# A decoder layer: weight and bias of the second layer norm applied by ScalarE on the transposed rows, and a written order from the cross-attention output to the first feed-forward group

## The chip, the cores and the metric

The kernel runs on one core of a Trainium2 chip. A core has a matrix engine (TensorE, PE in the profile, with PEld for its weight loads), VectorE (DVE), ScalarE (ACT), GpSimd (POOL) and SyncE (SP), which here issues the DMA transfers. Each engine works through its own queue in order; semaphores hold an instruction until what it reads is there. On chip there are SBUF, with 128 partitions, and PSUM, eight banks of 128 x 512 words, into which PE accumulates. The metric is the device time of one execution in microseconds (us), lower is better.

## What is computed

One layer of a decoder: a token mixer, a cross-attention, a feed-forward part, each followed by a layer norm over the sum with the scaled input. There are 256 tokens of 2048 features, all in float32.

```python
ALPHA = (2 * DEPTH) ** 0.25                       # DEPTH = 1
def layer_norm(x, g, b):
    mu = x.mean(-1, keepdims=True)
    var = jnp.square(x - mu).mean(-1, keepdims=True)
    return (x - mu) * lax.rsqrt(var + LN_EPS) * g + b

proj = x @ w_in                                   # 2048 -> 7176 columns
y = concat([mlstm_mixer(...), dilated_attention(...)]) @ w_out
x = layer_norm(ALPHA * x + y, ln_g[0], ln_b[0])
y = memory_cross_attention(x, mem, xq, xk, xv, xo)     # ends in o @ xo
x = layer_norm(ALPHA * x + y, ln_g[1], ln_b[1])
y = (silu(x @ w1) * (x @ w3)) @ w2                # hidden width 5632
x = layer_norm(ALPHA * x + y, ln_g[2], ln_b[2])
```

The change is about the second norm: the step from `o @ xo` to `x @ w1` and `x @ w3`.

## The kernel before, in words

**Products.** Each float32 factor is split into a high part (a cast to PE's fp32r, by ACT) and a low part (the difference to the original, by DVE): `split`, L109. A product is then three PE instructions: high by high, high by low part, low by high. One row of weights (a k-tile, 128 of the 2048 input features) is 128 x 1024; for a pair of rows one DMA brings a tile `w` (three of them in a ring, `RAW`), and the parts `wh`, `wl` go into rings of five (`SPLIT`) or into one of 34 numbered slots (`big`, given back by `free`). For 256 tokens (two halves m = 0, 1) and 1024 columns (two banks c) a row takes 2 x 6 products.

**gemm_seven** (L323) multiplies blocks with seven products in place of eight (sums of blocks are formed by `sums`, and `early` combines what they give). At its end it comes back to the `kept` rows: their products of the second token half are done last, so that the sums of the first half can begin sooner. **gemm_tokens** (L260) is the plain form, used for f0, the first 512 + 512 columns of w1 and w3. There the first six rows (`HEAD`) lie in slots, and the low parts of these are formed by POOL, in halves of 512 columns; PE does their products of token half 0, then those of half 1, and goes on with the others.

**The passage.** The output product of the cross-attention goes into z in two column halves, xo0 and xo1. `z[m][c]` are the rows (128 tokens x 512 columns, eight tiles; some of them have other names in the profile, such as `xk1r`). `Norm.add` adds a bank to z and takes the statistics, `Norm.finish` (L712) makes mean and scale (POOL does the power of -1/2), then two passes over the four tiles of z: L723 `(z - mean) * g`, L728 `* scale + b`. `put_transposed` (L735) then turns each tile into a PSUM bank (`x2p`) with four transposes (L739) and splits it into the operand `x2`, features by tokens: a cast by ACT, a difference by DVE (both L110/L111). z itself stays, as the input that the feed-forward part is added to much later (`w2_first`, L984, with scale ALPHA).

**After it.** f0's results go through `hidden` (L954: silu, product, transposes into `hT`); then come groups f2, f4, ... f20, each a `gemm_seven` over `x2`, whose results are put together by `whole` (L693, lines L696) before `hidden` takes them.

**Order.** Around the passage nothing is written by hand: the instructions of an engine are put in order by the framework's scheduler, which goes by a model of durations and by the buffers' rings. At the start of the program the same holds for the first stage, v0 (values of the mixer), beside which SP issues sixteen gathers of `rows`, a table of position biases.

Of the kernel before, what the change touches and what calls it, by code (L numbers as in the profile page):

```python
# [36 lines left out]
LAG, HEAD, LAG2 = 6, 6, 8  # L37
# [13 lines left out]
def decoder_layer(ctx: ExitStack, tc: tile.TileContext, A):  # L51
# [176 lines left out]
    def weights(src, n, name, load=None, kept=()):  # L228

        for b in range(n // 2):  # L230
# [13 lines left out]
            for i in range(2):  # L244
                at = 2 * b + i
                if load and n < KT:
                    load(at)
                if at in kept:
                    wh, wl = big(f"{name}h{at}"), big(f"{name}l{at}")
                else:  # L250
                    wh = wp.tile([P, W], F32R, tag="wh", name=f"{name}h{at}")
                    wl = wp.tile([P, W], F32R, tag="wl", name=f"{name}l{at}")
                eng = G if at in kept and kept[0] == 0 else V
                halves = (slice(0, 512), slice(512, 1024))
                for cs in halves if at in kept or first and i == 0 else (slice(0, 1024),):
                    SC.copy(wh[:, cs], w[:, i, cs])  # L256
                    eng.tensor_tensor(out=wl[:, cs], in0=w[:, i, cs], in1=as_f32(wh[:, cs]), op=ALU.subtract)  # L257
                yield at, wh, wl

    def gemm_tokens(op, src, nkt, name, order=None, kept=range(0), load=None, last=False):  # L260

        banks = [[bank(f"{name}b{m}{c}") for c in range(2)] for m in range(2)]
        order = order or list(range(nkt))

        def products(m, n, wh, wl, cols=range(2)):
            xh, xl = (op.get(order[n], x, m * P, P) for x in (0, 1))
            for c in cols:  # L270
                cs = slice(c * 512, (c + 1) * 512)
                T.matmul(banks[m][c], xh, wh[:, cs], start=n == 0, stop=False)  # L272
                T.matmul(banks[m][c], xh, wl[:, cs], start=False, stop=False)  # L273
            for c in cols:
                cs = slice(c * 512, (c + 1) * 512)
                T.matmul(banks[m][c], xl, wh[:, cs], start=False, stop=n == nkt - 1)  # L276

        behind = []
        for n, wh, wl in weights(src, nkt, name, load, kept):
            products(0, n, wh, wl)  # L280
            if n in kept:
                behind.append((n, wh, wl))
            else:
                products(1, n, wh, wl)
            if kept and n == kept[-1]:
                for c in range(2):
                    for i, wh, wl in behind:
                        products(1, i, wh, wl, (c,))
                for _, wh, wl in behind:
                    free(wh, wl)  # L290
            if last and n % 2 and n not in kept:
                op.free(order[n] // 2)
        if last:
            for n in kept:
                if n % 2:
                    op.free(order[n] // 2)
        return banks
# [25 lines left out]
    def gemm_seven(op, get, nkt, name, plan, early, order=None, kept=range(0), last=False):  # L323
# [49 lines left out]
        for c in range(2):  # L373
            for n, wh, wl in behind:
                tile_products(1, n, wh, wl, (c,))
        for n, wh, wl in behind:
            free(wh, wl)
            if last and n % 2:
                op.free(order[n] // 2)
# [272 lines left out]
    def add(m, g, banks, scale=ALPHA):  # L652
        for c in range(2):
# [39 lines left out]
    def whole(rows, banks):  # L693
        for m in range(2):
            for c in range(2):
                V.tensor_tensor(out=rows[m][c], in0=rows[m][c], in1=banks[m][c], op=ALU.add)  # L696

    class Norm:
# [7 lines left out]
        def add(self, m, g, banks, stats=True, scale=ALPHA):  # L706
            add(m, g, banks, scale)
            if stats:
                for c in (2 * g, 2 * g + 1):
                    V.bn_stats(out=self.st[m][:, c], in_=z[m][c])  # L710

        def finish(self, m, stats=False):  # L712
            if stats:
                for c in range(4):
                    V.bn_stats(out=self.st[m][:, c], in_=z[m][c])
# [4 lines left out]
            G.tensor_tensor(out=r[:, 1:2], in0=r[:, 0:1], in1=mhalf, op=ALU.pow)  # L720
            for c in range(4):
                t = z[m][c]
                V.scalar_tensor_tensor(  # L723
                    out=t, in0=t, scalar=mv[:, 0:1], in1=self.g[c], op0=ALU.subtract, op1=ALU.mult
                )
            for c in range(4):
                t = z[m][c]
                V.scalar_tensor_tensor(  # L728
                    out=t, in0=t, scalar=r[:, 1:2], in1=self.b[c], op0=ALU.mult, op1=ALU.add
                )  # L730

# [3 lines left out]
    def put_transposed(op, j0, m, t, name):  # L735

        pt = sbank(f"{name}p{j0}{m}")
        for i in range(4):
            T.transpose(pt[:, i * P : (i + 1) * P], t[:, i * P : (i + 1) * P], ident)  # L739
        for j in range(2):  # L740
            hi, lo = (x[:, :, m * P : (m + 1) * P] for x in op.views(j0 + j))
            split(hi, lo, pt[:, j * S : (j + 1) * S].rearrange("p (s t) -> p s t", s=2))
# [25 lines left out]
    nc.sync.dma_start(out=sel, in_=A["sel"])  # L768
    cw = const.tile([P, 16, 5], F32, tag="cw", name="cw")
# [350 lines left out]
```

## Time and profile before

| what | value |
|---|---|
| device time, median of 3 runs | 1546.54 us (1546.26 to 1547.52) |
| the profiled execution | 1546.63 us |
| its span, first to last instruction | 1544.8 us |
| instructions | 19283 |
| mean granted clock of PE | 0.995 |

The profile is that of one execution. A line of a timeline gives the start and the duration in microseconds, the engine, the source line and what is written from what, with the count of instructions that it stands for; in brackets is the idle time before it and what ended that. PE's durations overlap: a product counts from its start to its modelled end, and the next one starts before that. A line of a list of waits gives, after the colon, the time in total, the number and the longest. In a group line stand the least, the median and the greatest duration in ns. A granted clock of 1.00 is PE at full speed.

### The profile page before, as it was taken

The page shows a single profiled execution, that of the slowest core. Times are in us where ns is not written, and L with a number is a line of the kernel's source. Part 1 is how long each engine was busy: PE and PEld are TensorE (multiplying, and loading weights), DVE is VectorE, ACT ScalarE, POOL GpSimd, SP SyncE. Part 2 cuts the span into 40 slices and gives each one's busy share as a digit, 9 for nine tenths or more (in the row PEclk, how much of TensorE's full clock was granted, in tenths as well). Part 3 has the DMA queues.
Part 4 walks back from the last instruction along what each step waited for, and adds up shares of the span by engine and source line. Part 5 has one row for each costly group of instructions (what it writes and reads, how often), then busy time and mean ns, then how long its engine had stood idle before and what let it go on. Part 6 is the DMA issues. An engine that isn't in the chain of part 4 may idle for free.

```text
span 1544.8 us, 19283 instructions
## 1 busy us (share of the span) xinstructions
PE 1526.1 (99%) x7410; PEld 1277.2 (83%) x7410; DVE 1192.9 (77%) x1584; ACT 775.7 (50%) x1011; POOL 30.9 (2%) x30
## 2 busy tenths in 40 slices
PE   9999999999999999999999999999999999999997
PEld 7888888888888888888887888887788888888885
DVE  7665888787789655557788678887788878888897
ACT  5445555554544544444544554555445455555551
POOL 0000000000000000000014000000000000000000
PEclk9999999999999999999999999999999999999999
DMA  8674445674664546445553565665465656668552
GB/s 302 215 266 162 151 171 207 221 256 144 228 214 168 212 169 215 167 139 193 187 191 136 171 210 191 217 193 192 162 218 192 206 191 193 199 193 268 197 189 108
DMA packets 83354, 301.35 MB, mean 195 GB/s; under 512 B 7181, under 2 KB 9402, under 8 KB 59710
## 3 DMA queue, kind: packets, MB, share of 16 engines
q1 hardware_dynamic: 83262, 300.12, 56.3%
q8 instruction: 58, 0.95, 0.2%
q14 instruction: 34, 0.28, 0.1%
HBM read 297.97 MB, written 4.21 MB: 196 GB/s over the span
## 4 chain that ended last, share of the span: by engine, by line
PE 95%; DVE 3%; DMA 1%; issue 1%; ACT 0%; SPq 0%; DVEq 0%; ACTq 0%
PE w2a1P L338 2%; PE w2a0P L338 2%; PE w2b0P L338 2%; PE w2b1P L338 2%; PE f10P L338 2%; PE f20P L338 2%; PE v1P L338 2%; PE xo0P L338 2%; PE xo1P L338 2%; PE v0P L338 1%; PE f18P L338 1%; PE f8P L338 1%; PE wo0P L338 1%; PE f4P L338 1%; PE f2P L338 1%; PE f6P L338 1%
## 5 line engine op out<-in xcount | busy, mean ns | idle before, releaser
L257 DVE TENSOR_TENSOR xv1l<-xv1w,xv1h 128x1024 fp32r<-128x1024 f32 x16 | 19.6, 1224 | 20.7 <-ACT xv1h L256 20.6
L257 DVE TENSOR_TENSOR xv0l<-xv0w,xv0h 128x1024 fp32r<-128x1024 f32 x16 | 19.6, 1225 | 20.0 <-ACT xv0h L256 20.0
L110 ACT CAST w2a1h<-w2a1w 128x1024 fp32r<-128x1024 f32 (+1 forms) x24 | 22.5, 980 | 23.3 <-PE w2a1E L338 14.5
L110 ACT CAST w2a0h<-w2a0w 128x1024 fp32r<-128x1024 f32 (+1 forms) x24 | 22.8, 980 | 17.8 <-PE w2a0E L338 10.7
L111 DVE TENSOR_TENSOR w2a0l<-w2a0w,w2a0h 128x1024 fp32r<-128x1024 f32 (+1 forms) x24 | 26.5, 1131 | 6.1 <-ACT w2a0h L110 6.1
L111 DVE TENSOR_TENSOR w2a1l<-w2a1w,w2a1h 128x1024 fp32r<-128x1024 f32 (+1 forms) x24 | 26.4, 1131 | 5.6 <-ACT w2a1h L110 5.6
L256 ACT CAST xv1h<-xv1w 128x1024 fp32r<-128x1024 f32 x16 | 16.9, 1055 | 23.8 <-PE xv1b L276 17.2
L256 ACT CAST xv0h<-xv0w 128x1024 fp32r<-128x1024 f32 x16 | 16.9, 1055 | 21.6 <-PE xv0b L276 16.4
L110 ACT CAST w2b0h<-w2b0w 128x1024 fp32r<-128x1024 f32 (+1 forms) x20 | 19.2, 988 | 16.8 <-PE w2b0E L338 10.1
L338 PE MATMUL w2a0P<-w2a0h,hT 128*128 128x512 f32 x80 | 26.2, 391 | 0.2 <-ACT w2a0h L110 0.2
L257 POOL TENSOR_TENSOR f0l<-f0w,f0h 128x512 fp32r<-128x512 f32 x12 | 20.0, 1696 | 314.6 <-ACT f0h L256 314.6
L110 ACT CAST w2b1h<-w2b1w 128x512 fp32r<-128x512 f32 (+1 forms) x28 | 19.8, 758 | 12.5 <-PE w2b0E L338 5.4
L338 PE MATMUL w2a1P<-w2a1h,hT 128*128 128x512 f32 x80 | 25.4, 389 | 0.0
L110 ACT CAST wo1h<-wo1w 128x1024 fp32r<-128x1024 f32 (+1 forms) x16 | 15.6, 1000 | 18.9 <-PE wo1E L338 11.3
L110 ACT CAST f12h<-f12w 128x1024 fp32r<-128x1024 f32 (+1 forms) x16 | 15.6, 1000 | 18.7 <-PE f12E L338 11.3
L273 PE MATMUL f0b<-f0l,x 128*128 128x512 f32 x64 | 24.9, 405 | 0.1
L273 PE MATMUL xv0b<-xv0l,mT 128*128 128x512 f32 x64 | 25.0, 391 | 0.0
L111 DVE TENSOR_TENSOR w2b0l<-w2b0w,w2b0h 128x1024 fp32r<-128x1024 f32 (+1 forms) x20 | 22.2, 1139 | 3.6 <-ACT w2b0h L110 3.6
L272 PE MATMUL xv1b<-xv1h,mT 128*128 128x512 f32 x64 | 24.9, 392 | 0.0
L272 PE MATMUL xv0b<-xv0h,mT 128*128 128x512 f32 x64 | 24.9, 389 | 0.0
L273 PE MATMUL xv1b<-xv1l,mT 128*128 128x512 f32 x64 | 24.9, 389 | 0.0
L272 PE MATMUL f0b<-f0h,x 128*128 128x512 f32 x64 | 24.7, 407 | 0.0
(1641 smaller groups left out, 5488.4 us busy)
## 6 DMA issues: line engine op xcount, KB each, us to landing
w2a0w<-in_w SPq DMA_DIRECT2D x12, 1024.0 KB, 4.9
w2a1w<-in_w SPq DMA_DIRECT2D x12, 1024.0 KB, 5.2
w2b0w<-in_w SPq DMA_DIRECT2D x10, 1024.0 KB, 4.9
w2b1w<-in_w SPq DMA_DIRECT2D x10, 1024.0 KB, 5.0
v0w<-in_w_v SPq DMA_DIRECT2D x8, 1024.0 KB, 5.2
v1w<-in_w_v SPq DMA_DIRECT2D x8, 1024.0 KB, 4.9
v2w<-in_w_v SPq DMA_DIRECT2D x8, 1024.0 KB, 4.9
wo0w<-in_w_out SPq DMA_DIRECT2D x8, 1024.0 KB, 6.0
```

The source lines that it names most:

```text
L110: SC.copy(hi, src)
L111: V.tensor_tensor(out=lo, in0=src, in1=as_f32(hi), op=ALU.subtract)
L256: SC.copy(wh[:, cs], w[:, i, cs])
L257: eng.tensor_tensor(out=wl[:, cs], in0=w[:, i, cs], in1=as_f32(wh[:, cs]), op=ALU.subtract)
L272: T.matmul(banks[m][c], xh, wh[:, cs], start=n == 0, stop=False)
L273: T.matmul(banks[m][c], xh, wl[:, cs], start=False, stop=False)
L338: T.matmul(of[to], lhsT, rhs, start=to not in begun, stop=end)
```

## The change

- **Norm.** `Norm.bare` normalises z in one pass (`(z - mean) * scale`, one DVE instruction per tile). A small tile `lt` holds g and b with the features on the partitions; it is made at the start of the program by two loads, two PE transposes and a DVE copy. `scaled` lets ACT apply `lt` to the transposed tile, four activations of 128 x 128 from PSUM into a slot; ACT casts from there, and DVE takes the difference.
- **z.** Since z is then without g and b, `Norm.rest` multiplies and adds them on z later: 16 DVE instructions, which are to be issued after the last sum of `whole` of group f2.
- **Passage.** From the end of xo1 to f0's eighth row the order of PE, DVE and ACT is written by hand (`manual_schedule`). `gemm_seven` hands back the products of its kept rows as a generator (`behind`; a step is three products) so that the transposes can be put among them. The head has 8 rows, five of them in the rings. POOL has no subtractions any more.

The diff, cut to its core:

```diff
-LAG, HEAD, LAG2 = 6, 6, 8
+LAG, HEAD, POOLED, LAG2 = 6, 8, 5, 8
...
-                if at in kept:
-                    wh, wl = big(f"{name}h{at}"), big(f"{name}l{at}")
-                else:
-                    wh = wp.tile([P, W], F32R, tag="wh", name=f"{name}h{at}")
-                    wl = wp.tile([P, W], F32R, tag="wl", name=f"{name}l{at}")
-                eng = G if at in kept and kept[0] == 0 else V
+                wh = wp.tile([P, W], F32R, tag="wh", name=f"{name}h{at}")
+                wl = wp.tile([P, W], F32R, tag="wl", name=f"{name}l{at}")
                 halves = (slice(0, 512), slice(512, 1024))
-                for cs in halves if at in kept or first and i == 0 else (slice(0, 1024),):
-                    SC.copy(wh[:, cs], w[:, i, cs])
-                    eng.tensor_tensor(out=wl[:, cs], in0=w[:, i, cs], in1=as_f32(wh[:, cs]), op=ALU.subtract)
+                for cs in halves if first and i == 0 else (slice(0, 1024),):
+                    split(wh[:, cs], wl[:, cs], w[:, i, cs])
...
+    def token_products(op, banks, m, n, wh, wl, end):
+        xh, xl = (op.get(n, x, m * P, P) for x in (0, 1))
+        for c in range(2):
+            cs = slice(c * 512, (c + 1) * 512)
+            T.matmul(banks[m][c], xh, wh[:, cs], start=n == 0, stop=False)
+            T.matmul(banks[m][c], xh, wl[:, cs], start=False, stop=False)
+        for c in range(2):
+            cs = slice(c * 512, (c + 1) * 512)
+            T.matmul(banks[m][c], xl, wh[:, cs], start=False, stop=end)
+    def token_banks(name):
+        return [[bank(f"{name}b{m}{c}") for c in range(2)] for m in range(2)]
...
+        def rest():
+            for c in range(2):
+                for n, wh, wl in behind:
+                    yield tile_products(1, n, wh, wl, (c,))
             for n, wh, wl in behind:
-                tile_products(1, n, wh, wl, (c,))
-        for n, wh, wl in behind:
-            free(wh, wl)
-            if last and n % 2:
-                op.free(order[n] // 2)
+                free(wh, wl)
+                if last and n % 2:
+                    op.free(order[n] // 2)
+        if leave:
+            return banks, rest()
...
+        def bare(self, m, scales):
+            for t in z[m]:
+                V.tensor_scalar(
+                    out=t, in0=t, scalar1=scales[0], scalar2=scales[1], op0=ALU.subtract, op1=ALU.mult
                 )
+        def rest(self):
+            for c in range(4):
+                for m in range(2):
+                    t = z[m][c]
+                    V.tensor_tensor(out=t, in0=t, in1=self.g[c], op=ALU.mult)
+                    V.tensor_tensor(out=t, in0=t, in1=self.b[c], op=ALU.add)
...
+    def turn(m, t, name):
+        pt = sbank(name)
         for i in range(4):
             T.transpose(pt[:, i * P : (i + 1) * P], t[:, i * P : (i + 1) * P], ident)
+        return pt
+    def scaled(pt, j0, cols, name):
+        y = slot(name)
+        for i in range(4):
+            kt = 2 * j0 + i
+            SC.activation(
+                y[:, i * P : (i + 1) * P], pt[:, i * P : (i + 1) * P], ACT.Identity,
+                scale=cols[:, 0, kt : kt + 1], bias=cols[:, 1, kt : kt + 1],
+            )
+        return y
+    def parts_of(op, j0, m, y):
         for j in range(2):
             hi, lo = (x[:, :, m * P : (m + 1) * P] for x in op.views(j0 + j))
-            split(hi, lo, pt[:, j * S : (j + 1) * S].rearrange("p (s t) -> p s t", s=2))
+            yield hi, lo, y[:, j * S : (j + 1) * S].rearrange("p (s t) -> p s t", s=2)
...
+    lt, lrow, lp = const.tile([P, 2, KT], F32, tag="lt", name="lt"), slot("lrow"), sbank("ltp")
+    for i, x in enumerate(("ln_g", "ln_b")):
+        rows = lrow[:KT, i * P : (i + 1) * P]
+        nc.sync.dma_start(out=rows, in_=A[x][1].rearrange("c (i p) -> (c i) p", p=P))
+        T.transpose(lp[:, i * KT : (i + 1) * KT], rows, ident[:KT, :KT])
+    V.tensor_copy(lt.rearrange("p a k -> p (a k)"), lp[:, : 2 * KT])
+    free(lrow)
...
-    banks = gemm_seven(oT, fetch(A["xo"][1], "xo1"), KT, "xo1", plan, into_z(1, ALPHA), None, kept, True)
+    banks, behind = gemm_seven(
+        oT, fetch(A["xo"][1], "xo1"), KT, "xo1", plan, into_z(1, ALPHA), None, kept, True, leave=True
+    )
     x2 = Operand("x2")
-    for m in range(2):
-        ln.add(m, 1, banks, scale=1.0)
-        ln.finish(m)
-        for c in range(4):
-            put_transposed(x2, 2 * c, m, z[m][c], "x2")
-    ln.end()
+    f0, w0 = fetch(A["w13_tokens"], "f0"), {}
+    def upper(n):
+        if n % 2 == 0:
+            w0[n // 2] = f0(n // 2)
+        if n < POOLED:
+            wh, wl = (wp.tile([P, W], F32R, tag=f"w{x}", name=f"f0{x}{n}") for x in "hl")
+        else:
+            wh, wl = big(f"f0h{n}"), big(f"f0l{n}")
+        SC.copy(wh, w0[n // 2][:, n % 2])
+        return wh, wl
+    def lower(n):
+        wh, wl = head[n]
+        V.tensor_tensor(out=wl, in0=w0[n // 2][:, n % 2], in1=as_f32(wh), op=ALU.subtract)
+    def normal(m, c):
+        y = scaled(turns.pop((m, c)), 2 * c, lt, f"x2y{m}{c}")
+        p = list(parts_of(x2, 2 * c, m, y))
+        for hi, _, v in p:
+            SC.copy(hi, v)
+        ys[m, c] = y, p
+    def normal_low(m, c):
+        y, p = ys.pop((m, c))
+        for hi, lo, v in p:
+            V.tensor_tensor(out=lo, in0=v, in1=as_f32(hi), op=ALU.subtract)
+        free(y)
+    def step(n=1):
+        for _ in range(n):
+            next(behind, None)
+    def turn_in(m, c):
+        turns[m, c] = turn(m, z[m][c], f"x2p{m}{c}")
+    def head_products(m, *ns):
+        for n in ns:
+            token_products(x2, banks0, m, n, *head[n], False)
+    head, turns, ys = {}, {}, {}
+    with tc.manual_schedule(engines={mybir.EngineType.PE, mybir.EngineType.DVE, mybir.EngineType.Activation}):
+        for n in range(POOLED):
+            head[n] = upper(n)
+        for n in range(3):
+            lower(n)
+        step(6)
+        for c in range(2):
+            add(0, 1, banks, 1.0, (c,))
+            ln.stats(0, 2 + c)
+        r0 = ln.scales(0)
+        add(1, 1, banks, 1.0, (0,))
+        ln.stats(1, 2)
+        ln.bare(0, r0)
+        lower(3)
+        step(3)
+        for c in range(3):
+            turn_in(0, c)
+            step()
+            normal(0, c)
+        step(1)
+        normal_low(0, 0)
+        add(1, 1, banks, 1.0, (1,))
+        ln.stats(1, 3)
+        r1 = ln.scales(1)
+        normal_low(0, 1)
+        ln.bare(1, r1)
+        turn_in(0, 3)
+        banks0 = token_banks("f0")
+        head_products(0, 0, 1, 2)
+        lower(4)
+        turn_in(1, 0)
+        normal(1, 0)
+        normal_low(0, 2)
+        head[5] = upper(5)
+        head_products(0, 3, 4)
+        turn_in(1, 1)
+        normal(1, 1)
+        normal_low(1, 0)
+        lower(5)
+        normal(0, 3)
+        normal_low(1, 1)
+        normal_low(0, 3)
+        head_products(0, 5)
+        for n in (6, 7):
+            head[n] = upper(n)
+            lower(n)
+        turn_in(1, 2)
+        normal(1, 2)
+        normal_low(1, 2)
+        head_products(0, 6, 7)
+        turn_in(1, 3)
+        normal(1, 3)
+        normal_low(1, 3)
+        head_products(1, *range(HEAD))
+    for n in range(POOLED, HEAD):
+        free(*head[n])
+    for b in range(HEAD // 2, KT // 2):
+        for n, wh, wl in plain(f0, b, "f0"):
+            for m in range(2):
+                token_products(x2, banks0, m, n, wh, wl, n == KT - 1)
...
-    banks = gemm_tokens(x2, A["w13_tokens"], KT, "f0", kept=range(HEAD))
-    hidden(0, banks, lambda b, i: [x[:, i * 256 : (i + 1) * 256] for x in b], "f0")
+    hidden(0, banks0, lambda b, i: [x[:, i * 256 : (i + 1) * 256] for x in b], "f0")
...
+        done = whole(rows, banks)
         hidden(g, rows, lambda b, i: [b[i][:, x * 256 : (x + 1) * 256] for x in range(2)], f"f{g}")
         free(*rows[0], *rows[1])
+        if g == 2:
+            with tc.issue_after(done.ins):
+                ln.rest()
+            ln.end()
```

Three places of the order, each before and after, show what moves.

DVE at the end of group f2 (f2r, f2t and f2ru are its rows that are being put together; f4w, f4h, f4l the weights of the next group, their high and low parts), before:

```order
L962 TENSOR_TENSOR f2r_7660<-f2r_7660,x2r_7412 128x256
L696 TENSOR_TENSOR f2r_7660<-f2r_7660,f2E 128x512
L111 TENSOR_TENSOR f4l_7861<-f4w_7852,f4h_7860 128x512
L962 TENSOR_TENSOR f2t_7750<-f2t_7750,f2ru 128x256
L962 TENSOR_TENSOR f2r_7661<-f2r_7661,f2ru 128x256
L962 TENSOR_TENSOR f2t_7750<-f2t_7750,f2r_7660 128x256
L111 TENSOR_TENSOR f4l_7868<-f4w_7852,f4h_7867 128x1024
```

and after, where xk1r and z are tiles of z, xe and l1g in L736 the weight g, l1g and l1b in L737 the bias b:

```order
L684 TENSOR_TENSOR f2r_7689<-f2r_7689,f2E 128x512
L736 TENSOR_TENSOR xk1r_3523<-xk1r_3523,xe_6266 128x512
L736 TENSOR_TENSOR z_3535<-z_3535,xe_6266 128x512
...
L736 TENSOR_TENSOR z_3534<-z_3534,l1g_6312 128x512
L736 TENSOR_TENSOR z_3536<-z_3536,l1g_6312 128x512
...
L111 TENSOR_TENSOR f4l_7906<-f4w_7897,f4h_7905 128x512
L1091 TENSOR_TENSOR f2t_7779<-f2t_7779,f2ru 128x256
...
L737 TENSOR_TENSOR z_3534<-z_3534,l1b_6318 128x512
L737 TENSOR_TENSOR z_3536<-z_3536,l1b_6318 128x512
...
L111 TENSOR_TENSOR f4l_7913<-f4w_7897,f4h_7912 128x1024
```

Eight instructions of `rest` stand ahead of the first low part of f4 shown, and the other eight between it and the next.

ACT in the passage (x2p is the transposed tile in PSUM, x the parts of the operand x2, f0w and f0h a pair of weight rows and the high part of one), before:

```order
L110 CAST x_7019<-x2p_7014 128x2x128
L110 CAST x_7000<-x2p_6992 128x2x128
L110 CAST x_7011<-x2p_7003 128x2x128
L256 CAST f0h_7209<-f0w_7207 128x1024
L256 CAST f0h_7225<-f0w_7207 128x1024
L110 CAST x_7022<-x2p_7014 128x2x128
```

and after, from the first tile of the second token half to the eighth row of weights (x2y is the slot that the activations write):

```order
L754 ACTIVATE x2y_7025<-x2p_7110,lt 128x128 x4
L998 CAST x_7030<-x2y_7025 128x2x128
L998 CAST x_7031<-x2y_7025 128x2x128
L986 CAST f0h_7123<-f0w_6966 128x1024
L754 ACTIVATE x2y_7058<-x2p_7138,lt 128x128 x4
L998 CAST x_7046<-x2y_7058 128x2x128
L998 CAST x_7047<-x2y_7058 128x2x128
L754 ACTIVATE x2y_7058<-x2p_7082,lt 128x128 x4
L998 CAST x_7157<-x2y_7058 128x2x128
L998 CAST x_7158<-x2y_7058 128x2x128
L986 CAST f0h_7173<-f0w_7171 128x1024
L986 CAST f0h_7177<-f0w_7171 128x1024
```

Each tile has four more instructions on ACT, and the casts of weight rows 5, 6 and 7 (7123, 7173, 7177) stand behind named tiles: row 5 behind tile (1,0), that is token half 1, column group 0, rows 6 and 7 behind (1,1) and (0,3).

SP in stage v0 (v0w are pairs of weight rows of v0, i2w those of the next stage), before:

```order
L195 DMA v0w_803<-in_w_v 128x2048
L195 DMA v0w_837<-in_w_v 128x2048
L466 DMA i0r_316<-rows 128x256
L466 DMA i0r_316<-rows 128x128
L466 DMA i0t_310<-rows 128x256
...
L466 DMA tb_523<-rows 128x128
L243 DMA i2w_966<-in_w_qk 128x2048
```

and after:

```order
L195 DMA v0w_811<-in_w_v 128x2048
L454 DMA i0r_316<-rows 128x256
L454 DMA i0r_316<-rows 128x128
...
L454 DMA tb_523<-rows 128x128
L195 DMA v0w_845<-in_w_v 128x2048
L243 DMA i2w_974<-in_w_qk 128x2048
```

The eighth load of v0's weights (837 before, 845 after) stands behind the sixteen gathers instead of ahead of them.

More of the change, by code (lines that the diff above doesn't have):

```diff
@@ L226, in plain, with weights @@
             yield n, wh, wl
-    def weights(src, n, name, load=None, kept=()):
+    def weights(src, n, name, load=None):
         for b in range(n // 2):
@@ L297, in gemm_tokens @@
+    def gemm_tokens(op, src, nkt, name, load=None, last=False):
+        banks = token_banks(name)
+        for n, wh, wl in weights(src, nkt, name, load):
+            for m in range(2):
+                token_products(op, banks, m, n, wh, wl, n == nkt - 1)
+            if last and n % 2:
+                op.free(n // 2)
         return banks
@@ L321, in sums, with gemm_seven @@
         free(t, t2)
-    def gemm_seven(op, get, nkt, name, plan, early, order=None, kept=range(0), last=False):
+    def gemm_seven(op, get, nkt, name, plan, early, order=None, kept=range(0), last=False, leave=False):
         order = order or list(range(nkt))
@@ L372, in gemm_seven @@
                 op.free(order[2 * b] // 2)
-        for c in range(2):
+        def rest():
+            for c in range(2):
+                for n, wh, wl in behind:
+                    yield tile_products(1, n, wh, wl, (c,))
             for n, wh, wl in behind:
-                tile_products(1, n, wh, wl, (c,))
-        for n, wh, wl in behind:
-            free(wh, wl)
-            if last and n % 2:
-                op.free(order[n] // 2)
+                free(wh, wl)
+                if last and n % 2:
+                    op.free(order[n] // 2)
+        if leave:
+            return banks, rest()
+        for _ in rest():
+            pass
         return banks
@@ L650, in load_row, with add @@
         return out
-    def add(m, g, banks, scale=ALPHA):
-        for c in range(2):
+    def add(m, g, banks, scale=ALPHA, cols=range(2)):
+        for c in cols:
             t = z[m][2 * g + c]
@@ L695, in whole @@
             for c in range(2):
-                V.tensor_tensor(out=rows[m][c], in0=rows[m][c], in1=banks[m][c], op=ALU.add)
+                ins = V.tensor_tensor(out=rows[m][c], in0=rows[m][c], in1=banks[m][c], op=ALU.add)
+        return ins
     class Norm:
@@ L709, in add, with stats, scales @@
                 for c in (2 * g, 2 * g + 1):
[L710 to L715 removed]
+                    self.stats(m, c)
+        def stats(self, m, c):
+            V.bn_stats(out=self.st[m][:, c], in_=z[m][c])
+        def scales(self, m):
             mv = small.tile([P, 2], F32, tag="lmv", name=f"{self.name}mv{m}")
@@ L952, in decoder_layer @@
+    for n in range(POOLED, HEAD):
+        free(*head[n])
+    for b in range(HEAD // 2, KT // 2):
+        for n, wh, wl in plain(f0, b, "f0"):
+            for m in range(2):
+                token_products(x2, banks0, m, n, wh, wl, n == KT - 1)
     hT = Operand("hT")
```

46 lines of the change are left out of this document (8 added, 38 removed).

## Prediction

> **What bounds the kernel now.** I read the page first: the busy table, then the chain of work that ended last.
>
> ```profile
> span 1544.8 us, 19283 instructions
> PE 1526.1 (99%) x7410; PEld 1277.2 (83%) x7410; DVE 1192.9 (77%) x1584; ACT 775.7 (50%) x1011; POOL 30.9 (2%) x30
> PE 95%; DVE 3%; DMA 1%; issue 1%; ACT 0%; SPq 0%; DVEq 0%; ACTq 0%
> ```
>
> TensorE (PE) is busy 99% of the span and carries 95% of the chain. Whatever the change does to the other engines counts only where PE stands still for it, or works slowly after it. So the next view is the list of PE's waits, and there the stage that is rewritten.
>
> ```profile
> PE x2p L739 <- DVE xk1r L728: 2.3, 2, 1.3
> PE x2p L739 <- DVE z L728: 0.9, 1, 0.9
> PE f0b L276 <- DVE x L111: 0.4, 1, 0.4
> ```
>
> These three, 3.6 us, are the waits of the passage. The first two are transposes that wait for normalised rows, the third a product that waits for the low part of the operand. How long is the whole passage, and how much work is in it? PE's timeline answers.
>
> ```profile
> 802.10 0.39 PE L338 MATMUL xo1Q<-xo1h,oT 128*128 128x512 f32 x1
> ...
> 813.66 0.39 PE L338 MATMUL xo1E<-xo1h,oT 128*128 128x512 f32 x1
> 815.31 0.66 PE L739 MATMUL x2p<-ident,xk1r 128*128 128x128 f32 x4 [1.26 <-DVE xk1r L728]
> ...
> 843.00 0.60 PE L739 MATMUL x2p<-ident,z 128*128 128x128 f32 x4
> ...
> 859.81 0.61 PE L276 MATMUL f0b<-f0h,x 128*128 128x512 f32 x2
> ...
> 861.17 0.61 PE L276 MATMUL f0b<-f0h,x 128*128 128x512 f32 x2
> ...
> 868.42 0.39 PE L338 MATMUL f2P<-f2h,x 128*128 128x512 f32 x1
> ```
>
> From 802.10 to 868.42, where group f2 begins, are 66.3 us. By PE's rows the stretch holds 52 products of xo1 and 192 of f0 (16 rows of weights, 2 halves of the tokens, 6 products each). Six products take 861.17 − 859.81 = 1.36 us, one .2267, so 244 take 55.3. Eight groups of four transposes: .60 busy at 843.00, less the tail that the next overlaps (a product is busy .39 and .23 apart from the next, so .16), is .44 each, 3.5 together. Work 58.8, loss **7.5 us**: all that this passage can give. The three waits are half of it; the clock holds most of the rest.
>
> ```profile
> 814.00:817.36 3.36, 1.07 (x8) 0.79 (x8) 3.36 (x4) 2.36 (x5) 3.36 (x3) 1.00 0.43 124
> 817.36:820.78 3.42, 2.54 (x10) 1.96 (x9) 3.42 (x3) 0.74 (x2) 3.42 (x3) 0.50 0.44 184
> 820.78:824.20 3.42, 3.04 (x8) 1.85 (x7) 3.42 (x10) 2.35 (x4) 3.42 (x4) 0.50 0.48 144
> ```
>
> Columns of these windows: length, busy time of PE, PEld, DVE, ACT, POOL, PE's granted clock, DMA share. After 3.36 us in which PE worked 1.07, the clock is halved for 6.84 us, twice 3.42. A half-rate stretch of 3.42 us loses 1.7 us of work; this one lost about as much twice, 3.4 us. [...]
>
> **Part 1: the passage (gain).** What VectorE (DVE) carries here was dear because GpSimd (POOL) ran beside it.
>
> ```profile
> L723 DVE SCALAR_TENSOR_TENSOR xk1r<-xk1r,l1mv,xe x2: 743/744/746, 809.8 to 810.4; 128x512 f32<-128x512 f32 x2
> L723 DVE SCALAR_TENSOR_TENSOR z<-z,l1mv,xe x2: 1715/1749/1783, 825.0 to 826.6; 128x512 f32<-128x512 f32 x2
> L257 POOL TENSOR_TENSOR f0l<-f0w,f0h x12: 1265/1717/2352, 802.8 to 826.1; 128x512 fp32r<-128x512 f32 x12
> 221.97 0.42 DVE L811 TENSOR_SCALAR v1r<-v1r 128x512 f32<-128x512 f32 x1
> ```
>
> The same operation takes 744 ns alone and 1749 beside POOL's twelve subtractions. These go, and of 16 two-operand steps 8 one-operand steps remain: TENSOR_SCALAR of 128x512, between the .42 of the one at 221.97, less its overlap, and the .74 of the old step; I take .5, nearer to the row of the same kind. ScalarE (ACT) takes over weight and bias:
>
> ```profile
> 166.03 0.70 ACT L564 ACTIVATE g<-g,cols 128x128 f32<-128x128 f32 x2 [1.38 <-DVE cols L551]
> 166.63 0.39 ACT L565 ACTIVATE g<-g,cols 128x128 f32<-128x128 f32 x1
> 821.85 0.70 ACT L110 CAST x<-x2p 128x256 fp32r<-128x256 f32 x2 [1.65 <-DVE x L111]
> 822.45 2.00 ACT L256 CAST f0h<-f0w 128x1024 fp32r<-128x1024 f32 x2
> ```
>
> Two activations of 128x128 take .60 (166.03 to 166.63), two casts of 128x256 the same, a weight cast 1.0; a group (four activations, two casts) holds ACT for about 1.9. A weight difference on DVE takes 1.15 (busy 1.23 in the row at 920.64 below, less .08 of overlap: .68 busy there are .60 apart). I walk the new order with these, on before's clock:
> - PE has nine xo1 products left when it comes to the first transposes, at 811.85. DVE has three weight differences ahead of the adds, and ends the first normalised row at about 812.9: **wait (a), 1.1**.
> - PE: four groups of transposes and the nine products to 816.8, rows 0 to 2 of the weights for the first token half (18 products, 4.1) to 820.9, a group to 821.3, rows 3 and 4 to 824.0, a group to 824.5.
> - ACT: group (1,0) can begin at 821.3 and ends at 823.2, the cast of row 5 at 824.2, DVE's difference at 825.4. PE needs it at 824.5: **wait (b), .9**.
> - PE: row 5 to 826.6, a group to 827.0. ACT: groups (1,1) and (0,3) from 824.5 to 828.3, then the cast of row 6 to 829.3: **wait (c), 2.2**.
> - DVE's difference for row 6 comes at 830.5, one product after the cast: **wait (d), 1.0**.
> - Row 7 to 833.1, a group, then eight rows for the second token half (10.9) that need nothing new, and rows 8 to 15 (21.8): f2 begins at 866.2 to 866.4.
>
> Waits of 5.2 to 5.4 instead of a loss of 7.5: **−2.0**. Bounds: −6.3, if only (a) remains, and about +.3, if a group takes 2.5 on ACT instead of 1.9 ((b) sees one group, (c) three). What hides the first three groups' activations is the products of rows 0 to 2; without that cover each would cost PE its 1.9.
>
> **Part 2: `rest` in front of f4's low parts (loss).** The residual still needs weight and bias on z; 16 additions and multiplications of 128x512 now stand in DVE's order after f2's last sum, eight ahead of one low part of f4 and eight ahead of the next.
>
> ```profile
> 915.68 0.68 DVE L696 TENSOR_TENSOR f2r<-f2r,f2E 128x512 f32<-128x512 f32 x1
> 916.28 0.69 DVE L111 TENSOR_TENSOR f4l<-f4w,f4h 128x512 fp32r<-128x512 f32 x1
> 916.88 0.42 DVE L962 TENSOR_TENSOR f2t<-f2t,f2ru 128x256 f32<-128x256 f32 x1
> ...
> 920.64 1.23 DVE L111 TENSOR_TENSOR f4l<-f4w,f4h 128x1024 fp32r<-128x1024 f32 x1 [2.67 <-ACT f4h L110]
> ```
> ```profile
> 924.68 0.39 PE L338 MATMUL f4P<-f4l,x 128*128 128x512 f32 x1
> ```
>
> One costs .60 (915.68 to 916.28), sixteen 9.6. On before's clock DVE ends f2's sums at 916.28; 4.8 for the first lump, .6 for the low part, 1.1 for three short sums (916.88 to 917.97, where the idle time ahead of 920.64 begins), 4.8 for the second lump and 1.15 for the 128x1024 low part: 928.7. PE uses that low part at 924.68 in before; in the new order PE takes some products ahead of the transposes of `hidden`, and gets there at about 925.3. So PE waits 3.4, and DVE's later low parts cost another .5: **+3.9**. Both sides move 2.0 earlier with part 1, so the difference stays. The cover is DVE's idle 2.67 before 920.64 plus its lead over PE there (924.68 − 921.8, 2.9): 9.6 less 5.6 is 4.0, nearly the same from the other side. Nothing hides more, for DVE works without a pause around it. Bounds: 0, if DVE's lead is 4 us greater than read here, and 5 without the .6 of PE's new order.
>
> **Part 3: the start (loss).** Two small loads, two transposes and a DVE copy give the columns; PE's part is below the .45 of a group of four, so .3. But the eighth load of v0's weights also moves behind the sixteen gathers of `rows` in SyncE's (SP) order.
>
> ```profile
> 78.01 7.62 SPq L466 DMA_DIRECT2D tb<-rows  x12
> 85.73 10.17 SPq L243 DMA_DIRECT2D i2w<-in_w_qk  x4
> SPq L466 <- DMA v0w<-in_w_v: 2.0, 1, 2.0
> v0w<-in_w_v SPq DMA_DIRECT2D x8, 1024.0 KB, 5.2
> 90.41 0.39 PE L338 MATMUL v0P<-v0h,xT 128*128 128x512 f32 x1
> ```
>
> The gathers end at 85.73, or at 83.7 if the 2.0 us that SP waits for v0w in before fall away. Landing takes 5.2 and the cast 1.0, so the block is ready between 89.9 and 92.0, and a landing that takes 1 us longer among the gathers makes it 93. PE comes to it at 90.41, with the new transposes a little later: a wait of 0 to 2.2, taken as .2 because the row nearest, the median landing, gives it. Part 3: **+.5**.
>
> **Part 4: the clock.** A wait that empties a third or more of a stretch has halved the clock once in before. Two places can do it now: wait (c), with its neighbours (b) and (d), and f4's 3.4 us. Each costs 1.7 if the stretch falls badly, and neither surely does; the likeliest count is one of the two: **+1.7**. [...]
>
> **Sum.** The profiled execution took 1546.63 us (span 1544.8 plus 1.8 around it), .1 above the median of the runs, 1546.54. 1546.63 − 2.0 + 3.9 + .5 + 1.7 = 1550.7. What a measurement of this kernel tells from no change is about 0.2%, 3.1 us: 1543.5 to 1549.6 counts as the same.
>
> **Rivals.**
> 1. *No clock stretch at all*: 1549.0. [...] Against: the 1.07 busy in 3.36 above. Chance .17, same.
> 2. *The lumps are hidden.* If DVE comes to f2's last sum 4 us earlier against PE than the rows show, part 2 costs nothing: 1546.63 − 2.0 + .5 = 1545.1. Against: DVE's low parts wait for ACT's casts, and these for buffers that PE frees, so the lead can hardly grow. Chance .10, same.
> 3. *The passage closes better than I walk it*: only (a) stays, a gain of 6.3; with f4's wait 1544.7, with a stretch of clock there 1546.4. For: (b) to (d) rest on ACT's activations as measured from SBUF, while these read PSUM. Chance .09, same.
> 4. *The other side: ACT and DVE run further ahead of PE*, through the passage and up to f4, because no step of theirs is slowed by POOL any more. Then (b) to (d) vanish and `rest` falls into DVE's lead: 1546.63 − 6.3 + .5 = 1540.8. One point decides it: DVE's idle time and lead before f4's low part must be 9.6 us or more when `rest` begins; the rows give 5.6. Chance .14, faster.
> 5. *The eighth load is late in full*: +2.2 at v0, 1552.9. Chance .05, slower.
>
> That the passage still waits at every group, so that the written order changes nothing, is the bound +.3 of part 1; it gives 1553.0 and is counted with the forecast. The forecast, with one stretch or two (1550.7, 1552.4), has .45.
>
> **Range.** 1544.5 to 1553.2 takes in all but case 4 (.14) and a little of the tails. Faster .14; same .17 + .10 + .09 = .36; slower .45 + .05 = .50. Forecast's own range: 1549.7 to 1552.6.
>
> **What would show it.** Right: PE's list of waits has low parts of f4 for DVE with about 3.4 us; the first transpose of the passage still waits 1.1; f0's sixth to eighth rows wait for ACT's casts; f2 starts 64.3 us after the xo1Q product named above; the steps of the norm take .4 to .6 on DVE; v0's eighth block waits under 1 us; one or two stretches of clock .50 in the passage or at f4. Wrong: f4's first products of that block run through (part 2 falls), or f2 starts after under 61 us (part 1 was too pessimistic), or no stretch of half clock appears.

## The result, and the profile after

The changed kernel takes 1553.58 us in the median of five executions (1550.49 to 1554.83), the kernel before 1546.54. The ratio is 1.0039, with a 95% interval of 1.0028 to 1.005: slower by about 6 us. The profiled execution is the slowest of the five, 1554.83, with a span of 1552.7.

The page and PE's list of waits of the changed kernel:

```profile
span 1552.7 us, 19308 instructions
PE 1529.6 (99%) x7412; PEld 1279.9 (82%) x7412; DVE 1196.0 (77%) x1599; ACT 786.6 (51%) x1037; POOL 10.2 (1%) x18
PE 92%; DVE 4%; DMA 2%; ACT 1%; SPq 1%; issue 0%; DVEq 0%; ACTq 0%
```
```profile
PE f4P L318 <- DVE f4l L111: 2.8, 1, 2.8
PE f0b L260 <- ACT f0h L986: 2.1, 1, 2.1
...
PE v0P L318 <- ACT v0h L110: 1.5, 1, 1.5
...
PE f0b L261 <- DVE f0l L991: 1.4, 2, 0.8
...
PE x2p L746 <- DVE xk1r L728: 0.2, 1, 0.2
```

PE's share is still 99%, but its share of the chain has gone from 95 to 92%, and DVE, DMA, ACT and SP have what it lost. The transposes hardly wait for the norm any more (.2 in place of 3.2). In their place stand a wait for v0's last weights, waits for f0's weight rows, and the wait for f4's low part. DVE and PE at this last wait, with four of `rest`'s additions ahead of the low part:

```profile
927.60 2.49 DVE L737 TENSOR_TENSOR z<-z,l1b 128x512 f32<-128x512 f32 x4
930.01 1.22 DVE L111 TENSOR_TENSOR f4l<-f4w,f4h 128x1024 fp32r<-128x1024 f32 x1
```
```profile
931.28 0.79 PE L318 MATMUL f4P<-f4l,x 128*128 128x512 f32 x1 [2.81 <-DVE f4l L111]
```

Where did the time go? A stage lasts here from PE's first product of one tile to its first of the next: v0 to i2, xo1 to f2 (the passage), f4 to f6. From the timelines, in us:

| kernel | v0 | passage | f4 | median of the runs | ratio to before, 95% |
|---|---|---|---|---|---|
| before | 43.93 | 96.77 | 43.11 | 1546.54 | |
| the change | 46.38 | 97.18 | 49.41 | 1553.58 | 1.0039 (1.0028 to 1.0050) |
| e1 | 45.90 | 97.74 | 43.11 | 1546.13 | 1.0000 (.9991 to 1.0009) |
| e2 | 43.93 | 95.76 | 47.00 | 1552.20 | 1.0038 (1.0025 to 1.0051) |
| e3 | 46.48 | 90.01 | 47.74 | 1545.59 | .9989 (.9980 to .9998) |
| e4 | 44.44 | 94.72 | 47.89 | 1550.22 | 1.0020 (1.0011 to 1.0029) |
| e5 | 45.44 | 96.69 | 43.10 | 1547.24 | 1.0001 (.9992 to 1.0009) |
| e6 | 43.93 | 99.24 | 43.11 | 1549.11 | 1.0012 (1.0002 to 1.0021) |
| e7 | 43.93 | 90.08 | 43.12 | 1544.59 | .9984 (.9976 to .9993) |
| e8 | 44.45 | 90.56 | 43.12 | 1545.78 | .9992 (.9983 to 1.0001) |
| e9 | 43.93 | 90.06 | 43.11 | 1540.82 | .9959 (.9946 to .9971) |
| e10 | 43.93 | 90.32 | 43.12 | 1544.06 | .9978 (.9969 to .9987) |
| e11 | 45.54 | 90.21 | 43.14 | 1541.80 | .9962 (.9949 to .9976) |

The stages are those of the one profiled execution of each kernel; a profile can be far from the median (those of the change and of e1 are the slowest of their executions). Each ratio is to executions of before that were measured beside the kernel; their median was 1547.1 to 1547.5 in the later measurements, so between rows the ratios are compared and not the medians. For the change the three stages differ from before by +2.5, +.4 and +6.3, and the stages between and behind them give back some 1.3, which nothing here explains.

Half-rate stretches lie in two of these stages. The windows below (length, busy time of PE, PEld, DVE, ACT, POOL, granted clock, DMA share, GB/s) are cut at the changes of the clock in this profile, at 831.43, 838.25, 930.41 and 937.24, and at steps of 3.41 us from them, first in the passage, then in f4:

```profile
828.01:831.43 3.42, 1.34 (x8) 0.90 (x7) 3.10 (x10) 3.42 (x9) 0.00 (x0) 1.00 0.85 307
831.43:834.84 3.41, 2.79 (x7) 1.88 (x7) 2.92 (x4) 3.21 (x8) 0.00 (x0) 0.50 0.18 26
834.84:838.26 3.42, 3.42 (x12) 2.73 (x11) 2.26 (x7) 0.00 (x0) 0.00 (x0) 0.50 0.72 275
927.00:930.41 3.41, 1.31 (x7) 0.56 (x4) 3.41 (x7) 1.92 (x4) 0.00 (x0) 1.00 0.00 0
930.41:933.83 3.42, 2.54 (x6) 2.06 (x7) 3.42 (x4) 0.43 (x1) 0.00 (x0) 0.50 0.41 108
933.83:937.24 3.41, 3.41 (x9) 2.64 (x9) 3.41 (x6) 1.66 (x2) 0.00 (x0) 0.50 0.63 213
```

Each time a window with PE busy 1.3 of 3.4 us is followed by two windows at half rate. Before had one such stretch of two windows, in the passage (817.37 to 824.20), and none at f4. The passage in PE's timeline, with its waits, and DVE's first normalising steps:

```profile
804.13 0.39 PE L318 MATMUL xo1Q<-xo1h,oT 128*128 128x512 f32 x1
...
814.26 0.66 PE L746 MATMUL x2p<-ident,xk1r 128*128 128x128 f32 x4 [0.23 <-DVE xk1r L728]
...
827.27 0.50 PE L261 MATMUL f0b<-f0l,x 128*128 128x512 f32 x1 [0.76 <-DVE f0l L991]
...
831.22 0.64 PE L260 MATMUL f0b<-f0h,x 128*128 128x512 f32 x1 [2.08 <-ACT f0h L986]
832.48 0.79 PE L261 MATMUL f0b<-f0l,x 128*128 128x512 f32 x1 [0.62 <-DVE f0l L991]
...
870.91 0.39 PE L318 MATMUL f2P<-f2h,x 128*128 128x512 f32 x1
```
```profile
813.68 0.99 DVE L728 TENSOR_SCALAR xk1r<-xk1r,l1mv,l1r 128x512 f32<-128x512 f32 x2
```

### The profile page after: what moved, and what is told of

Same layout as the page of the kernel before. It is cut to its first block, busy times and chain, and to the rows that moved or that the text cites. A ratio compares the mean times of both kernels' runs of the same rounds, so it can differ in the third digit from the quotient of the medians.

```text
span 1552.7 us, 19308 instructions
## 1 busy us (share of the span) xinstructions
PE 1529.6 (99%) x7412; PEld 1279.9 (82%) x7412; DVE 1196.0 (77%) x1599; ACT 786.6 (51%) x1037; POOL 10.2 (1%) x18
## 4 chain that ended last, share of the span: by engine, by line
PE 92%; DVE 4%; DMA 2%; ACT 1%; SPq 1%; issue 0%; DVEq 0%; ACTq 0%
PE w2a1P L318 2%; PE w2a0P L318 2%; PE w2b0P L318 2%; PE w2b1P L318 2%; PE f10P L318 2%; PE v1P L318 2%; PE wo0P L318 1%; PE f14P L318 1%; PE f16P L318 1%; PE f18P L318 1%; PE f20P L318 1%; PE wo1P L318 1%; PE f8P L318 1%; PE f6P L318 1%; PE f12P L318 1%; PE v2P L318 1%
## 5 line engine op out<-in xcount | busy, mean ns | idle before, releaser
L111 DVE TENSOR_TENSOR v0l<-v0w,v0h 128x1024 fp32r<-128x1024 f32 (+1 forms) x16 | 18.2, 1153 | 15.7 <-ACT v0h L110 15.7
L110 ACT CAST v0h<-v0w 128x1024 fp32r<-128x1024 f32 (+1 forms) x16 | 15.5, 997 | 25.7 <-DMA v0w<-in_w_v 8.3
L110 ACT CAST w2b0h<-w2b0w 128x1024 fp32r<-128x1024 f32 (+1 forms) x20 | 19.2, 987 | 17.0 <-PE w2b0E L318 10.1
L110 ACT CAST f4h<-f4w 128x1024 fp32r<-128x1024 f32 (+1 forms) x16 | 15.9, 998 | 20.4 <-PE f4E L318 8.9
```

The source lines that it names most:

```text
L110: SC.copy(hi, src)
L111: V.tensor_tensor(out=lo, in0=src, in1=as_f32(hi), op=ALU.subtract)
```

## The experiments

**e1: without `rest`.**

```diff
-            with tc.issue_after(done.ins):
-                ln.rest()
             ln.end()
```

> Leaves out the 16 multiplications and additions of weight and bias on z, so the residual of the feed-forward part lacks them. If those 16 instructions are what f4's first products wait for, the wait of 2.8 us for f4's low part goes, and with it the half-clock stretch at 930; the time falls from 1553.6 by 2.8 to 6.2 us, to 1547.4 to 1550.8. Rival: the low part is late for another reason (ACT's casts or the loads of f4's weights); then a wait of over 1.5 us stays at the same product and the time falls by under 1.5.

Stage f4 takes 43.11 us, as before to the hundredth; no wait for f4l is left and no stretch at half rate there. The ratio falls from 1.0039 to 1.0000, some 6 us, near the upper end of what was expected; the median of 1546.13 lies 1.3 below the expected range. The rival is out: the low part was late for the sixteen instructions alone. The profile, with its passage of 97.74, is that of the slowest of eleven executions, 1549.99 (granted clock .996); the fastest took 1544.88 (.998).

**e2: the columns made late.** The block that makes `lt` stands just ahead of `ln = Norm(1, "l1")`.

```diff
-    lt, lrow, lp = const.tile(...), slot("lrow"), sbank("ltp")
...
+    lt, lrow, lp = const.tile(...), slot("lrow"), sbank("ltp")
     ln = Norm(1, "l1")
```

> The columns of weight and bias are made just before the second norm instead of at the start. If the start's loss is the eighth load of v0 behind the gathers, PE's wait of 1.5 us for v0h goes, i2's first product comes at about 96.5 instead of 98.9, and the time falls by 2.3, to about 1551.3, since the two loads and transposes cost under 0.5 in their new place. Rival: the loss is the price of the two loads, two transposes and the copy themselves; then it moves with them, and the time stays within 1 us of 1553.6.

The wait for v0h is gone and stage v0 takes 43.93 again, but the ratio, 1.0038, is that of the change. The gain of 2.3 that was expected is not seen in the time of this pair: 1.4 by the medians, .2 by the ratios. Its executions spread from 1550.61 to 1556.62, and the clean pair for this question is e9 and e11.

**e3: ACT's casts first.** Tile (0,3) right behind (0,2) on ACT, the casts of rows 5 to 7 ahead of the second token half. DVE's order changes with it: the differences of rows 5 to 7 come ahead of, or between, those of the second token half.

```diff
         turn_in(0, 3)
+        normal(0, 3)
+        for n in (5, 6, 7):
+            head[n] = upper(n)
         banks0 = token_banks("f0")
...
-        head[5] = upper(5)
...
+        lower(5)
+        normal_low(0, 3)
+        lower(6)
         normal_low(1, 0)
-        lower(5)
-        normal(0, 3)
+        lower(7)
         normal_low(1, 1)
-        normal_low(0, 3)
         head_products(0, 5)
-        for n in (6, 7):
-            head[n] = upper(n)
-            lower(n)
```

> In the passage ACT takes tile (0,3) right behind (0,2), then the casts of weight rows 5, 6 and 7, and only then the tiles of the second token half. If PE's waits at rows 5 to 7 come from ACT's order, their 3.5 us fall under 1, no half-clock stretch is left in the passage, and f2 starts 3 to 7 us earlier against the start of the passage: 1546.5 to 1550.5. Rival: ACT is simply full there (15 us of activations and casts for the tiles); then the waits move to the tiles of the second half, 2 to 4 us of them remain, and the time stays above 1551.5.

PE waits for nothing between 800 and 870 us; the passage takes 90.01, 7.2 less than in the change and 6.8 less than before. ACT's timeline shows the order that does it:

```profile
821.18 1.58 ACT L754 ACTIVATE x2y<-x2p,lt 128x128 f32<-128x128 f32 x4
822.56 0.79 ACT L998 CAST x<-x2y 128x256 fp32r<-128x256 f32 x2
823.17 3.03 ACT L986 CAST f0h<-f0w 128x1024 fp32r<-128x1024 f32 x3
826.02 1.59 ACT L754 ACTIVATE x2y<-x2p,lt 128x128 f32<-128x128 f32 x4
```

All three rows are cast by 826.2, and the tiles of the second half follow back to back, 1.98 us each, while PE does not wait. So ACT was not full; it had the urgent casts behind work that could wait. How much of the gain is due to DVE's new order is not told apart here. The time fell further than expected, to .9989 of before.

**e4: the wait filled.** The four transposes of tile (1,2) are done five times in place of once.

```diff
         turn_in(1, 2)
+        for _ in range(4):
+            for i in range(4):
+                T.transpose(turns[1, 2][:, i * P : (i + 1) * P], z[1][2][:, i * P : (i + 1) * P], ident)
```

> PE repeats the four transposes of tile (1,2) four times, 1.8 us of work of no use in the 2.1 us wait for row 6. Nothing else changes, so without an effect on the clock the time is that of the changed kernel plus 0 to 0.3. If the half-clock stretch follows from PE's idleness in the passage, it is gone there, the products behind it run at .2267 again, and the passage ends about 3 us earlier in an execution that had the stretch: median 1550.5 to 1552. Rival: the stretch has another trigger; it is still in the profile at about 831 and the median stays at 1553 to 1554.5.

Useless work made the kernel faster: the ratio is 1.0020 in place of 1.0039 (the two intervals just touch), the median 1550.22, slightly below what was expected, and the passage 94.72 in place of 97.18. The windows on the grid show why:

```profile
824.34:827.76 3.42, 2.66 (x16) 1.93 (x15) 2.48 (x4) 3.26 (x11) 0.00 (x0) 1.00 0.28 60
827.76:831.17 3.41, 2.28 (x18) 1.73 (x16) 3.09 (x9) 3.41 (x8) 0.00 (x0) 1.00 0.62 250
831.17:834.58 3.41, 3.41 (x17) 2.82 (x18) 3.14 (x6) 2.26 (x8) 0.00 (x0) 1.00 0.40 106
```

The worst window has PE busy 2.28 of 3.41, where the change had one of 1.34 of 3.42, and the clock stays at 1.00. The extra transposes are all that the edit adds, so here the stretch followed from PE's idleness.

**e5: the columns alone, in the kernel before.** The block of `lt` at the start of the kernel before; nothing uses it.

> The kernel before, with the columns of weight and bias made at the start and then not used; norm, passage and residual are the old ones. If the start's loss belongs to this part, the eighth load of v0 stands behind the gathers, PE waits 1 to 2 us for v0h unless the load happens to land early, and the time is 0.5 to 2.5 above that of the kernel before, median about 1548.6. Rival: the loss needs the rest of the change (other slots, another order in v0); then the time stays within 0.5 of the kernel before and v0 shows no wait.

Between theory and rival. The eighth load is issued at 84.10, in before at 72.30, so this block alone moves it. In the profile v0 does wait (.6) and its stage takes 1.5 longer; in the time there is no difference to before (1.0001).

**e6: POOL's subtractions on DVE, in the kernel before.**

```diff
-                eng = G if at in kept and kept[0] == 0 else V
+                eng = V
```

> The kernel before, with the low parts of f0's first six weight rows on DVE in place of POOL, nothing else. If the written order is what the passage needs, this alone does little: DVE's norm steps fall to 744 ns (5.4 us in sum), twelve subtractions of 0.6 come to it (7.2 us), PE's waits at the transposes stay between 2 and 5 us and the time within 2 us of the kernel before. Rival: POOL beside DVE was the passage's loss; then the waits fall below 1.5 us, no half-clock stretch is left and the time falls by 3 us or more.

The norm's steps fall to the 744 ns that they have elsewhere, as the group line shows, and the kernel gets slower (1.0012): PE waits 5.4 us once, for the low part of a turned tile that now stands behind twelve subtractions on DVE.

```profile
L723 DVE SCALAR_TENSOR_TENSOR z<-z,l1mv,xe x2: 742/744/745, 831.2 to 831.9; 128x512 f32<-128x512 f32 x2
```
```profile
824.38 1.22 PE L276 MATMUL f0b<-f0h,x 128*128 128x512 f32 x2 [5.40 <-DVE x L111]
```

Freeing DVE of POOL is not by itself enough; with e3's order the waits are gone.

**e7 and e8: all three edits, and without the late columns.** `rest` in four pieces, g and b loaded again for each in place of the norm's own rows (e9's form, with `{2: (0,), 4: (1,), 6: (2,), 8: (3,)}`), e3's order, in e7 also e2's place for `lt`.

> The changed kernel with three edits: the columns made just before the second norm, ACT's casts ahead as in e3, and weight and bias put on z in four pieces of four instructions behind the last sums of f2, f4, f6 and f8, with the rows loaded again for each piece. If the three losses are separate, none of the three waits is left, no half-clock stretch falls between 800 and 960, and the time is 1546.6 less 7.0 (the passage as e3 had it) plus about 0.5 to 1: 1539.5 to 1541.5. Rival: DVE is too full in the groups behind f2, or the new loads come in the way; then waits for low parts of f4 to f10 appear and the time is above 1543.

> As e7, with the columns at the start as in the change. If the start costs what the waits show, PE waits for v0h again in most executions, and the time is 1 to 2.3 above e7. Rival: the start's loss is caught up later in the mixer, whose stages have slack; then e7 and e8 agree within 0.7.

e7 is 3 us or more above what was expected. All three losses are gone, as the table shows, and f10 begins 6.0 us earlier than in before; then PE waits 3.0 us in f10, where before waited .4, with a window at half rate behind it. e8 is 1.2 above e7, at the lower end of what was expected; in its profile PE does not wait for v0h, and stage v0 is .5 longer.

**e9, e10 and e11: fewer pieces.**

```diff
         if g == 2:
-            with tc.issue_after(done.ins):
-                ln.rest()
             ln.end()
+        for c in {2: (0, 1), 4: (2, 3)}.get(g, ()):
+            gt, bt = slot(f"rg{c}"), slot(f"rb{c}")
+            for t, src in ((gt, "ln_g"), (bt, "ln_b")):
+                nc.sync.dma_start(out=t, in_=A[src][1][c : c + 1, :].to_broadcast([P, 512]))
+            with tc.issue_after(done.ins):
+                for m in range(2):
+                    V.tensor_tensor(out=z[m][c], in0=z[m][c], in1=gt, op=ALU.mult)
+                    V.tensor_tensor(out=z[m][c], in0=z[m][c], in1=bt, op=ALU.add)
+            free(gt, bt)
```

That is e9; e10 has `{2: (0,), 4: (1,), 6: (2, 3)}`, e11 is e9 with the columns at the start.

> As e7, but weight and bias go on z in two pieces of eight instructions, behind the last sums of f2 and f4, so that nothing is added near f10. Eight cost 4.8 us, under the 5.6 us of idle time and lead that DVE has before f4's low part in the profile of the kernel before. If that cover is what decides, PE waits for no low part of f4 or f6, no half-clock stretch falls between 800 and 1060, and the time is 1540 to 1541.5. Rival: the cover is smaller than read, a wait of 1 us or more stays at f4 or f6 and the time is above 1542.

> As e7, but the pieces are four, four and eight instructions behind f2, f4 and f6. If e7's wait of 3.0 us at f10 came from the last piece's loads and instructions in front of f10, it is gone and the time is that of e9, within 0.7. Rival: the wait at f10 belongs to the earlier start of f10 against its weights; then e9 and e10 both show it, and the time is 1543 to 1545.

> As e9, with the columns at the start as in the change: the clean pair for the start. If the start costs what it cost in the profile of the change, the time is 1.5 to 2.3 above e9; if a part is caught up, or the load often lands in time, 0 to 1.2.

e9 is what the reasons asked for: no wait and no stretch at half rate in the passage, f4 or f6 (granted clock .998 in its profile, .995 in that of before), 1540.82 us, .9959 of before (.9946 to .9971), faster than both kernels. Eight instructions, 4.8 us, fit under the cover of 5.6; sixteen did not. e11 is .98 above e9.

e10 was expected to equal e9 and is 3.2 above it; the wait has moved to f8, the group behind its last piece. DVE, ACT and PE in e10's timelines:

```profile
1006.33 0.69 DVE L292 TENSOR_TENSOR f8s<-f8t,f8w 128x512 f32<-128x512 f32 x1
1006.94 0.68 DVE L111 TENSOR_TENSOR hTm<-rb,hTm 128x512 fp32r<-128x512 f32 x1
1007.54 0.68 DVE L293 TENSOR_TENSOR f8s<-f8s,f8w 128x512 f32<-128x512 f32 x1
```
```profile
1008.26 1.04 ACT L110 CAST f8h<-f8s 128x1024 fp32r<-128x1024 f32 x1 [1.91 <-DVE f8s L293]
```
```profile
1009.36 0.50 PE L318 MATMUL f8Q<-f8h,x2m 128*128 128x512 f32 x1 [1.60 <-ACT f8h L110]
```

PE waits for a cast, the cast for a sum of weights (f8s), and this sum stands on DVE behind the eight instructions and behind the steps of `hidden`, where e9 has it formed before f6's last two sums. In e7's f10 the same sum (f10s, at 1051.54) is as late. Why the scheduler puts it there behind f6 and f8 and not behind f4 stays open.

## Why the prediction was right, and where it was off

The direction and the places were right: slower, by an uncovered lump at f4, a late load at the start, and a passage whose waits move from the norm to ACT's casts. The forecast of 1550.7 is 2.9 below the measured median, which lies .4 above the end of the range. The 1.3 us that other stages gave back stand in no part of the prediction; without this luck the miss would have been larger.

**Part 1, the waits: right. The term: wrong.** By the idle times in the profile (a) came out .2 in place of 1.1: PE comes to the first transposes when the walk had it, 9.75 us behind the xo1Q product, but DVE ends the first normalised row about 10.1 us behind that product, where the walk had 10.8. The others are (b) .76 for .9, (c) 2.08 for 2.2, (d) .62 for 1.0. One normalising step took .54 (.5 taken), a tile on ACT 1.98 (1.9 taken). But f2 starts 66.8 us after that product, where 64.3 was forecast and before had 66.3: in the profiled execution the passage did not gain 2.0, it lost .4. The step that failed is "Waits of 5.2 to 5.4 instead of a loss of 7.5": the 7.5 held before's stretch of clock, 3.4, and the 5.3 held none, so the −2.0 counts on a stretch that goes away. It came back, though the waits were walked rightly; nothing in Part 1 says why it should not, with 5.3 of waits against about 4.1. Like for like, Part 1 should have read about +1 and left the clock to Part 4, whose single stretch had to stand for this one and for f4's. The executions of e1 agree, where passage and start are left: the ratio is 1.0000 (.9991 to 1.0009), where −2.0 and +.5 alone give .9990 and one stretch of 1.7 more gives 1.0001.

**Part 4: the mis-sized term.** It took one stretch of 1.7 for passage and f4 together, and both places had theirs. With two the sum is 1552.4, the prediction's own second figure; the ratio of 1.0039 makes 1552.6 of before's 1546.54. In the profiled execution each of the two was two windows long, 13.7 us at half rate where before had 6.8. That execution is the slowest. An estimate for the median one from its granted clock, .995: half rate for twice .005 of 1551.4 us, 15.5 us, of which 7.9 lie behind PE's last product as in the profile; about two windows are left, as many as before had. What a stretch cost was not always the same: stage f4 takes 47.00 in e2 with the clock at 1.00 behind the wait, 47.74 in e3, where a window at .50 begins at 925.55, and 49.41 with two windows at .50. The changed kernel's times spread over 4.3 us, before's over 1.3 beside it (up to 3.0 later), and the granted clock roughly goes with them: .997 in the fastest execution, .995 in the median one, .993 in the slowest. Rival 1, no stretch at all, does not fit the median. And before's window, from which Part 4 took its measure, was not a third empty but two thirds (1.07 busy of 3.36).

**Part 2: right.** The stage without a stretch is +3.9 (47.00 − 43.11 in e2), as forecast, and the price is `rest` and nothing else (e1). The parts differ: a wait of 2.7 in e2 (2.8 in the change) and 1.2 behind it, for 3.4 and .5, so the exact sum is in part luck. The 4.8 us of e9's eight instructions fit under the cover of 5.6; by the wait that the 9.6 of sixteen leave, the cover was nearer 6.8. Rivals 2 and 4 asked for a lead that did not come: with the passage 6.8 faster in e3, f4 still waits 2.3.

**Part 3: too small in the profile, about right in the time.** The load was issued at 84.09, as walked, and its cast, which waited for it, began at 91.88, nearly 8 us later, against the 5.2 taken:

```profile
84.09 0.38 SPq L195 DMA_DIRECT2D v0w<-in_w_v  x1
```
```profile
91.88 2.00 ACT L110 CAST v0h<-v0w 128x1024 fp32r<-128x1024 f32 x2 [8.32 <-DMA v0w<-in_w_v]
```

PE waited 1.5 and stage v0 grew by 2.5, so rival 5 came true in this execution. With the columns at the start the growth was .5 in two profiles (e4, e8) and 1.5 to 2.6 in the others; the wait depends on when the load lands. In the time the pairs give, by the medians, 0 (e5), 1.0 (e9, e11), 1.2 (e7, e8) and 1.4 (e2 and the change, .2 by the ratios), none of them clear of its interval: a cost near 1 us is likely, not proved.

**Rival 3** was the one that an edit could make true: the waits (b) to (d) were not a matter of ACT's speed, as argued there, but of the order on it and on DVE (e3).

## What to carry to other kernels

Work that is taken off the critical path has to be put down somewhere: compare it with the idle time and lead of its engine at exactly that place, and split it to fit. Where several engines feed PE, put on each queue what PE needs next ahead of what it needs later; a handful of entries moved on ACT and DVE took 7 us off the passage here. And when a loss is compared with a forecast, keep the clock's part out of both or in both.

## What the runs showed of the hardware

In the profiles of before and of the change the granted clock was 1.00 or .50, and its changes lie whole multiples of 3.413 us apart: in before at 817.37, 824.20 and 1537.59, the second 2 and the third 211 times 3.413 behind the first; in the change at 831.43, 838.25, 930.41, 937.24 and 1544.81, the others 2, 29, 31 and 209 times behind the first. The windows below are cut at such steps. They give the time in which the trace has PE busy, in us of 3.41 or 3.42 (of 3.36 in the one of before at 814.00), with the profile and the start of the window, and what the clock did in the next:

| | followed by half rate | clock unchanged |
|---|---|---|
| full-rate windows | .72 (e2, 828.68), 1.07 (before, 814.00), 1.31 and 1.34 (the change, 927.00 and 828.01), 1.50 (e3, 922.14), 1.71 (e7, 1051.93) | 1.64 (e2, 927.66), 1.88 (the change, 90.74), 1.93 (e7, 1048.52), 2.28 (e4, 827.76) |

| | next still at half rate | next at full rate |
|---|---|---|
| half-rate windows | 2.54 (before, 817.36), 2.54 and 2.79 (the change, 930.41 and 831.43) | 3.04 (before, 820.78), 3.41 and 3.42 (the change, 933.83 and 834.84) |

At the ends of the programs the clock fell too, after .28 (before, 1534.17) and .96 (the change, 1541.39). The length of the wait alone did not decide it here: at f4 PE waited 2.7 us in e2, and the clock stayed at 1.00; it waited 2.3 in e3 and 2.8 in the change, and half rate followed. The two full-rate windows of the table that come closest to each other with different outcomes, of e2 and of e7:

```profile
927.66:931.08 3.42, 1.64 (x7) 1.38 (x8) 3.42 (x4) 0.41 (x1) 0.00 (x0) 1.00 0.14 18
931.08:934.49 3.41, 3.25 (x15) 2.32 (x14) 3.41 (x6) 1.70 (x2) 0.00 (x0) 1.00 0.85 287
```
```profile
1051.93:1055.35 3.42, 1.71 (x6) 1.13 (x7) 2.25 (x3) 3.03 (x4) 0.00 (x0) 1.00 0.55 158
1055.35:1058.76 3.41, 3.41 (x9) 2.64 (x9) 2.74 (x4) 2.42 (x3) 0.00 (x0) 0.50 0.64 200
```

At 1.64 of 3.42 the clock held, at 1.71 it fell, so these busy times do not separate the two outcomes sharply; they end where PE's products are modelled to end. In e4 1.8 us of extra transposes, by the estimate made before the run, in a wait of 2.1 made the passage 2.5 us shorter.
